# A hybrid attention and Fourier block on one core: the ninth group of the input projection in the order of the others, its chain buffers made earlier, short groups in five accumulators, first-stage raw loads spread

## The chip, the cores and the metric

The kernel runs on one core of a Trainium2 chip. The core has TensorE (PE, matrix products into PSUM banks), VectorE (DVE), ScalarE (ACT), GpSimd (POOL) and SyncE (SP); they run side by side and wait for one another by semaphores. DMA transfers are asked on the queues of SP, ACT and POOL and are carried out by 16 DMA engines that all queues share. The metric is the device time of one execution in microseconds; less is better.

## The reference

One layer of a diffusion block in fp32: 512 latent tokens, 256 context tokens, width 2048.

```python
shift, scale, gate = split(silu(c) @ w_ada + b_ada, 3)          # shift_c, scale_c alike from c_ctx
h  = rmsnorm(x, norm_g) * (1 + scale) + shift                    # 512 x 2048
hc = rmsnorm(ctx, norm_g) * (1 + scale_c) + shift_c              # 256 x 2048
p  = h @ w_in                                                    # 2048 -> 9216: q, k, v, za, ub, zb, ga, gb
kc, vc = (hc @ w_in[:, k and v])                                 # context keys and values
q, k = rope(rmsnorm(q)), rope(rmsnorm(k))
attn = attention(q, [k, kc], [v, vc])                            # 12 query heads, 4 key heads
y_a  = (attn * silu(za)) @ w_proj_a
y_b  = (fft2(ub) * silu(zb)) @ w_proj_b                          # FNet, real part
y    = (sigmoid(ga) * y_a + sigmoid(gb) * y_b) @ w_out
out  = rmsnorm(x + gate * y, final_g)
```

## The kernel before

All products run in three passes: each fp32 weight is split into a high and a low part (`whi` by ACT, line 181, `wlo` by DVE, line 182), and `mm3` (lines 337 to 339) adds hi·hi, hi·lo and lo·hi in PSUM. A raw weight tile (`wr`, 128 x 1024, 0.5 MB) is loaded to one of a few raw slots, split, and used by 12 matmuls; that is a *piece*, and four pieces are a *product*.

The input projection is done in groups of 1024 columns, each as a Winograd form of Strassen's 2x2 scheme with seven products (`PRODUCTS`): P1, Q5, P2, Q6, P7, Q3, Q4. `ORDER` is U (the ninth group, which holds ub and zb), 0 to 2 (queries), 3 and 4 (gates), 5 (keys and values, with the context's), 6 and 7 (gates). The right-hand sides of P1, Q5, Q6 and Q4 are running sums of the four blocks of the weight: w00, then + w01, + w11, + w10. They lie in four *chain* buffers R0 to R3, one for each piece. w00 is loaded plainly, w01 is loaded raw and added by DVE (line 266), w11 and w10 are added by accumulating DMA transfers on POOL's queue (line 287) as soon as the chain's former state has been split. P7's right-hand side is a raw w00 minus the chain (DVE, line 272). P2 and Q3 take raw tiles as they are.

Groups 3, 6 and 7 (`EARLY`) are *short*: what depends on P1 and P2 alone was computed in the first stage, so that they have five products, and their chain's w00 was loaded ahead.

A product's four pieces add up in a pair of PSUM banks. PSUM has room for two pairs under the name `x` and two under `y`. In U the pair `x` takes P1 and then P2 on top of it, and `y` takes Q5 and then Q6, with a copy by ACT between (lines 875 and 880). At the end of a product `early_end` (short groups) or the code above it combines pairs, copies and results.

The first stage computes the modulation vectors from w_ada (`wa` tiles of 1 MB, line 490, on POOL's queue), the norm of x, and h in 16 row blocks kb; x lies in a tile `xt`. Between the blocks TensorE runs the early work for the short groups; its raw tiles are asked on ACT's queue (`load_more`, with `may` as the number that may be asked), and `form_row` (lines 641 to 650) makes the first forms of x for kb from 8 on. `warm` issues matmuls that nobody reads. When the stage is over, `xt`'s pool is closed, the chain buffers are made in its room, and POOL asks their w00 for U (line 738).

The order of TensorE's work is that of the program. On the other engines a scheduler orders the work; `issue_after` pins one instruction behind another. `look` and the raw slots set how far ahead a piece is asked and split; `get` asks for more whenever a piece is used.

In Q4 of the last group TensorE also transposes the keys of the first head (line 1167), into a pair `x`.

## Time and profile before

| what | us |
|---|---|
| median of 3 runs | 1374.88 (1367.93 to 1375.35) |
| the profiled execution | 1372.4 |
| its span | 1370.6 |
| TensorE busy | 1295.0 (94%) |
| DVE busy | 1008.1 (74%) |
| ACT busy | 704.1 (51%) |
| mean granted TensorE clock | 0.983 |

The first stage ends near 152 us, and U near 239; groups 0 to 2 run to about 466, group 3 to about 530, group 4 to 605, group 5 to 740, group 6 to 801, group 7 to 857. The Fourier branch, attention and the output projections follow.

A row of a timeline has the start, the length, the engine, the line, the operation, what it writes and reads, the shapes, and in brackets how long the engine had been idle before it and what ended that. A row of windows has for each engine the busy time and the number of instructions, the granted clock (1.00 is full), the busy share of the DMA engines, and GB/s.

### The profile page before, as it was taken

Reading aid. Unit: us, or ns where it says so; the run is one execution under the profiler, and the core shown is the slowest. Engines: PE = TensorE matmul, PEld = TensorE weight load, DVE = VectorE, ACT = ScalarE, POOL = GpSimd, SP = SyncE. Lnnn points to the kernel's source line nnn. Section 1 sums busy time; section 2 is a strip of 40 time slices with the busy share of each in tenths; the row PEclk is TensorE's granted clock in tenths of the full one; section 3 lists DMA queues with packets and bytes.
Section 4 is the critical chain, followed back from the end, with each engine's and each line's share of the span. In section 5 each row is a group of like instructions: output and inputs, shape, how many; then the busy total and the mean of one; then the engine's idle time right before and its main releaser. Section 6 shows DMA issues by size and latency. Waiting matters only on the chain.

```text
span 1370.6 us, 17532 instructions
## 1 busy us (share of the span) xinstructions
PE 1295.0 (94%) x6444; PEld 1047.1 (76%) x6444; DVE 1008.1 (74%) x1307; ACT 704.1 (51%) x1120; POOL 195.1 (14%) x273
## 2 busy tenths in 40 slices
PE   6889989999999989999999898999999999999997
PEld 4555668888888868878887676788888888888885
DVE  3447688678888778856767578588888867978676
ACT  4343544555555535444333445476766644665544
POOL 0111010101111120100102111001110122121210
PEclk9999999999999999999999999999999999999999
DMA  9999878788988887988788997437873599998985
GB/s 384 416 350 419 291 195 253 191 254 215 255 227 254 304 221 242 291 283 223 194 283 240 264 291 220 179 105 230 261 269 123 156 267 230 241 235 223 215 214 169
DMA packets 109623, 338.46 MB, mean 247 GB/s; under 512 B 10465, under 2 KB 33633, under 8 KB 105441
## 3 DMA queue, kind: packets, MB, share of 16 engines
q0 software_dynamic: 34464, 138.96, 41.9%
q1 hardware_dynamic: 47712, 158.01, 32.4%
q10 hardware_dynamic: 27360, 40.38, 8.1%
q8 instruction: 50, 0.82, 0.2%
q14 instruction: 37, 0.30, 0.1%
HBM read 300.60 MB, written 36.71 MB: 246 GB/s over the span
## 4 chain that ended last, share of the span: by engine, by line
PE 73%; DMA 9%; DVE 8%; issue 5%; ACT 3%; POOL 1%; SPq 0%; ACTq 0%; DVEq 0%; POOLq 0%
PE banks L337 10%; PE banks L338 10%; PE banks L339 10%; PE x L338 6%; PE x L337 6%; PE x L339 6%; PE y L337 5%; PE y L338 5%; PE y L339 5%; DMA R<-in_w_g 3%; DMA wr<-in_w_g 3%; PE banks L1397 2%; PE pd L597 2%; DVE wlo L182 2%; DMA wa<-in_w_ss 1%
## 5 line engine op out<-in xcount | busy, mean ns | idle before, releaser
L182 DVE TENSOR_TENSOR wlo<-wr,whi 128x1024 fp32r<-128x1024 f32 (+1 forms) x130 | 157.5, 1214 | 81.9 <-ACT whi L181 81.6
L181 ACT ACTIVATE whi<-R 128x1024 fp32r<-128x1024 f32 x133 | 140.5, 1059 | 144.4 <-PE banks L339 47.2
L182 DVE TENSOR_TENSOR wlo<-R,whi 128x1024 fp32r<-128x1024 f32 x133 | 162.1, 1223 | 60.3 <-ACT whi L181 59.9
L181 ACT ACTIVATE whi<-wr 128x1024 fp32r<-128x1024 f32 (+1 forms) x130 | 136.4, 1051 | 129.3 <-PE y L339 38.6
L337 PE MATMUL banks<-whi,s 128*128 128x512 f32 x396 | 157.8, 399 | 3.2 <-DVE s L1232 2.2
L338 PE MATMUL banks<-wlo,s 128*128 128x512 f32 x396 | 155.9, 394 | 0.0
L339 PE MATMUL banks<-whi,s 128*128 128x512 f32 x396 | 155.8, 394 | 0.0
L338 PE MATMUL x<-wlo,s 128*128 128x512 f32 x360 | 143.0, 397 | 8.7 <-DVE wlo L182 8.7
L337 PE MATMUL x<-whi,s 128*128 128x512 f32 x360 | 142.3, 395 | 2.6 <-ACT whi L181 2.0
L339 PE MATMUL x<-whi,s 128*128 128x512 f32 x360 | 141.8, 394 | 0.0
L287 POOL DMA_DIRECT2D R<-in_w_g x72 | 61.8, 862 | 465.4 <-DVE wlo L182 266.9
L337 PE MATMUL y<-whi,s 128*128 128x512 f32 x304 | 119.6, 393 | 7.5 <-ACT ev L880 6.8
L339 PE MATMUL y<-whi,s 128*128 128x512 f32 x304 | 119.0, 392 | 0.6 <-DVE s L182 0.6
L338 PE MATMUL y<-wlo,s 128*128 128x512 f32 x304 | 119.1, 392 | 0.4 <-DVE wlo L182 0.4
L181 ACT ACTIVATE s<-wr 128x512 fp32r<-128x512 f32 (+3 forms) x105 | 67.8, 671 | 72.1 <-DMA wr<-cf_d 22.8
L181 ACT ACTIVATE s<-R 128x512 fp32r<-128x512 f32 (+1 forms) x94 | 60.6, 663 | 61.5 <-DMA R<-in_w_g 18.9
L182 DVE TENSOR_TENSOR s<-wr,s 128x512 fp32r<-128x512 f32 (+3 forms) x105 | 75.9, 746 | 22.0 <-ACT s L181 21.4
L337 PEld LDWEIGHTS banks<-whi,s 128*128 128x128 f32 x396 | 75.0, 189 | 18.7 <-issue 2.6
L338 PEld LDWEIGHTS x<-wlo,s 128*128 128x128 f32 x360 | 68.8, 191 | 25.0 <-DVE wlo L182 10.9
L339 PEld LDWEIGHTS banks<-whi,s 128*128 128x128 f32 x396 | 74.9, 189 | 15.8
L338 PEld LDWEIGHTS banks<-wlo,s 128*128 128x128 f32 x396 | 75.1, 190 | 14.1 <-DVE wlo L182 0.2
L182 DVE TENSOR_TENSOR s<-R,s 128x512 fp32r<-128x512 f32 (+1 forms) x94 | 67.1, 734 | 21.4 <-ACT s L181 21.3
(291 smaller groups left out, 2829.3 us busy)
## 6 DMA issues: line engine op xcount, KB each, us to landing
wr<-in_w_g SPq DMA_DIRECT2D x131, 512.0 KB, 5.4
R<-in_w_g POOLq DMA_DIRECT2D x88, 512.0 KB, 7.4
wa<-in_w_ss POOLq DMA_DIRECT2D x26, 1024.0 KB, 11.3
wr<-in_w_gate SPq DMA_DIRECT2D x32, 512.0 KB, 5.5
wr<-in_w_o SPq DMA_DIRECT2D x24, 512.0 KB, 7.9
R<-in_w_o POOLq DMA_DIRECT2D x24, 512.0 KB, 9.1
wr<-in_w_early ACTq DMA_DIRECT2D x21, 512.0 KB, 9.5
R<-in_w_g SPq DMA_DIRECT2D x20, 512.0 KB, 5.2
```

The source lines that it names most:

```text
L181: first = nc.scalar.activation(hi, src, ACT.Copy)
L182: return first, nc.vector.tensor_tensor(lo, src, hi.bitcast(F32), op=ALU.subtract)
L287: nc.gpsimd.dma_start(chain[e.pc], e.nxt, accum_op=ALU.add)
L337: nc.tensor.matmul(o, ah, bh, start=start, stop=False, skip_group_check=cont)
L338: nc.tensor.matmul(o, ah, bl, start=False, stop=False, skip_group_check=cont)
L339: nc.tensor.matmul(o, al, bh, start=False, stop=stop, skip_group_check=cont)
L597: nc.tensor.matmul(acc[32 * j : 32 * j + 32, :256], c2[:, n, :], w[:, k, :], start=h == 0 and k < 4, stop=h == 1 and k > 3)
L1397: nc.tensor.transpose(tp[:, k * P : (k + 1) * P], p[:, k * P : (k + 1) * P], ident)
```

## The change

1. U takes the order of the other groups, with P2 behind Q5. The forms that are split in U (`between`) move with it. Its P1 becomes a piece of stage 0 like the others, whose w00 goes straight to the chain buffer.
2. `xt` becomes two tiles, rows 0 to 3 and 8 to 11 in the pool `xa`, the others in `pa`. At kb 12 `xa` is closed and the chain buffers are made in its room. Their w00 for U is asked on SP's queue behind the last use of `xa`'s rows, in kb 11, and behind two raw tiles for P2 of U, which come first on that queue. POOL's four loads at the end of the stage are gone.
3. Short groups run Q3, Q5, Q6, P7, Q4, each in a pair of its own (Q3, Q6 and Q4 in `x`, Q5 and P7 in `y`). `early_end` takes six DVE operations in place of five and two ACT copies. w10 goes to the chain behind P7's subtraction. The loads for the Fourier branch move along, and the context's tokens in group 3 are worked on in the four pieces of Q6 in place of every other piece of Q3 and Q5.
4. In the first stage the raws that a row block asks are pinned behind that block's ACT operation and are no longer counted one by one. Two raw loads that ACT had asked at 0.7 us, for pieces used at kb 11, go with the others of kb 8. Eight warming matmuls stand at the start and none within the first modulation. `wacc`, where they write, is another bank.

```diff
 OUT_GROUP = ("P1", "P2", "Q5", "Q6", "P7", "Q3", "Q4")
-EARLY_GROUP = ("Q3", "Q5", "P7", "Q6", "Q4")
+EARLY_BANK = {"Q3": "a", "Q5": "b", "Q6": "d", "P7": "c", "Q4": "a"}
+EARLY_GROUP = ("Q3", "Q5", "Q6", "P7", "Q4")
...
-    return EARLY_GROUP if g in EARLY else OUT_GROUP if g == U else ONE_GROUP
+    return EARLY_GROUP if g in EARLY else ONE_GROUP
...
-    if n % 2 == 0 and 0 <= n < 8:
-        return "cn", n // 2
+    if 8 <= n < 12:
+        return "cn", n - 8
...
-                stream(key, [w[a, b, pc] for a, b in what], 1024, 2, pc=r, nxt=part(3) if off and g not in EARLY else None,
-                       off=off)
-            elif (name, g) == ("P1", U):
-                stream(key, [part(0)], 1024, 2, pc=r)
+                stream(key, [w[a, b, pc] for a, b in what], 1024, 2, pc=r, nxt=part(3) if off else None, off=off)
...
-                elif name == "Q6" and g in EARLY:
-                    todo[-1].nxt = part(3)
...
+        if kb == CHAIN_AT:
+            xa.close()
+            rc = ctx.enter_context(tc.tile_pool(name="rc", bufs=1, reuse_waits="tile"))
+            chain.extend(rc.tile([P, 1024], F32, name=f"R{pc}") for pc in range(4))
+        return ins
...
+        warm(8)
         norm_first()
         modulate(0)
-        warm(1)
         columns(0)
...
-                used = sum(r for a in ahead for r in [len(a.raws)])
-                may[0] = sum(p[1] for p in raw_pools) - used
-                load_more()
-                assert not may[0], (kb, may[0])
+                may[0] = 8
+                with tc.issue_after(act):
+                    load_more()
+                may[0] = 0
...
-    for pc in range(4):
-        nc.gpsimd.dma_start(chain[pc], w_g[len(KINDS)][0, 0, pc])
-        left[pc] = 1
...
-            if name == "Q5":
-                self.Y = self.new()
-                nc.scalar.copy(self.Y, a)
+            if name == "Q6":
+                sub(self.X, a, self.X)
+                self.V, self.Y = self.new(), self.new()
+                add(self.V, self.acc["b"], self.X)
+                add(self.Y, self.acc["a"], self.V)
+                self.done(0, 1, self.Y, self.Y)
             elif name == "P7":
-                self.V = self.new()
-                nc.scalar.copy(self.V, a)
-            elif name == "Q6":
+                sub(self.V, self.V, a)
+                self.done(1, 1, self.V, self.V)
                 sub(self.X, a, self.X)
-                sub(self.V, self.X, self.V)
-                self.done(1, 1, self.V, self.V)
-                sub(self.Y, self.X, self.Y)
-                nc.vector.tensor_tensor(self.X, self.acc["a"], self.X, op=ALU.add)
-                self.done(0, 1, self.X, self.X)
             elif name == "Q4":
...
-                    sub(self.Y[:, t, :], a[:, t, :], self.Y[:, t, :])
-                self.done(1, 0, self.Y, self.Y)
+                    add(self.X[:, t, :], a[:, t, :], self.X[:, t, :])
+                self.done(1, 0, self.X, self.X)
```

On TensorE in U, the last matmuls of the product ahead of Q6 and the first of Q6, before (`x` and `y` are pairs of banks, `s_240` and the like are split weights or forms of x; the numbers tell tiles apart, and lines are one or two further in the changed kernel):

```order
L338 MATMUL y_1465<-s_370,s_1372 128x512
L339 MATMUL y_1465<-s_369,s_1373 128x512
L337 MATMUL y_1465<-s_369,s_1372 128x512
L338 MATMUL y_1465<-s_370,s_1372 128x512
L339 MATMUL y_1465<-s_369,s_1373 128x512
L337 MATMUL y_1465<-whi_1490,s_1528 128x512
L338 MATMUL y_1465<-wlo_1491,s_1528 128x512
```

The same place in the changed kernel:

```order
L338 MATMUL x_1300<-s_377,s_1178 128x512
L339 MATMUL x_1300<-s_378,s_1178 128x512
L340 MATMUL x_1300<-s_377,s_1179 128x512
L338 MATMUL x_1300<-s_377,s_1178 128x512
L339 MATMUL x_1300<-s_378,s_1178 128x512
L340 MATMUL x_1300<-s_377,s_1179 128x512
L338 MATMUL y_1387<-whi_1490,s_1528 128x512
L339 MATMUL y_1387<-wlo_1491,s_1528 128x512
```

Before, Q6 follows Q5 in the same pair; now P2 stands ahead of it, in the other pair.

On DVE in group 6, from the last addition to the chain for Q5 on, before (L272 is P7's subtraction, `R_1278` to `R_1281` are the chain buffers):

```order
L266 TENSOR_TENSOR R_1281<-R_1281,wr_5516 128x1024
L272 TENSOR_TENSOR wr_5536<-R_1278,wr_5536 128x1024
L182 TENSOR_TENSOR wlo_5520<-R_1281,whi_5519 128x1024
L272 TENSOR_TENSOR wr_5555<-R_1279,wr_5555 128x1024
L182 TENSOR_TENSOR wlo_5540<-wr_5536,whi_5539 128x1024
L272 TENSOR_TENSOR wr_5574<-R_1280,wr_5574 128x1024
L182 TENSOR_TENSOR wlo_5559<-wr_5555,whi_5558 128x1024
```

The same place now (L273 is the subtraction, `R_1060` to `R_1063` the chain):

```order
L267 TENSOR_TENSOR R_1063<-R_1063,wr_5518 128x1024
L183 TENSOR_TENSOR wlo_5522<-R_1063,whi_5521 128x1024
L183 TENSOR_TENSOR wlo_5541<-R_1060,whi_5540 128x1024
L183 TENSOR_TENSOR wlo_5559<-R_1061,whi_5558 128x1024
L183 TENSOR_TENSOR s_249<-R_1062,s_248 128x2x256
L183 TENSOR_TENSOR s_378<-R_1062,s_377 128x2x256
L273 TENSOR_TENSOR wr_5538<-R_1060,wr_5538 128x1024
L183 TENSOR_TENSOR s_498<-R_1063,s_497 128x2x256
L183 TENSOR_TENSOR s_651<-R_1063,s_650 128x2x256
L183 TENSOR_TENSOR wlo_5613<-wr_5538,whi_5612 128x1024
```

Q6's four splits of the chain come first now, and P7's subtractions behind them.

On TensorE in group 7, around the transposes of the keys (`ident`), before and then now:

```order
L339 MATMUL x_5980<-whi_6175,s_907 128x512
L337 MATMUL x_5980<-whi_6175,s_906 128x512
L1167 MATMUL x_6158<-ident,wr_6052 128x128 x6
L338 MATMUL x_5980<-wlo_6176,s_906 128x512
L339 MATMUL x_5980<-whi_6175,s_907 128x512
```

```order
L339 MATMUL y_6076<-s_378,s_1462 128x512
L340 MATMUL y_6076<-s_377,s_1463 128x512
L1169 MATMUL x_6161<-ident,wr_6051 128x128 x6
L338 MATMUL x_6182<-s_497,s_782 128x512
L339 MATMUL x_6182<-s_498,s_782 128x512
```

They stood within Q4's second piece and stand between P7 and Q4 now.

68 lines of the change are left out of this document (37 added, 31 removed).

## The prediction

> **What bounds the kernel now.** I read the page first (shares, the chain that ended last), then TensorE's timeline for every pause longer than 0.2 us, then for each pause the engine that ended it, then windows and the DMA view.
>
> ```profile
> span 1370.6 us, 17532 instructions
> PE 1295.0 (94%) x6444; PEld 1047.1 (76%) x6444; DVE 1008.1 (74%) x1307; ACT 704.1 (51%) x1120; POOL 195.1 (14%) x273
> PE 73%; DMA 9%; DVE 8%; issue 5%; ACT 3%; POOL 1%; SPq 0%; ACTq 0%; DVEq 0%; POOLq 0%
> ...
> R<-in_w_g POOLq DMA_DIRECT2D x88, 512.0 KB, 7.4
> ```
>
> TensorE is the bound, and time can only come from its pauses. These are the ones that the change touches:
>
> ```profile
> 164.22 0.50 PE L337 MATMUL x<-s,s 128*128 128x512 f32 x1 [1.10 <-ACT ev L875]
> 193.07 0.79 PE L337 MATMUL y<-whi,s 128*128 128x512 f32 x1 [6.80 <-ACT ev L880]
> 499.75 0.79 PE L337 MATMUL x<-s,s 128*128 128x512 f32 x1 [5.79 <-ACT s L181]
> 763.92 0.79 PE L338 MATMUL x<-wlo,s 128*128 128x512 f32 x1 [5.73 <-DVE wlo L182]
> 821.51 0.50 PE L338 MATMUL x<-wlo,s 128*128 128x512 f32 x1 [1.23 <-DVE wlo L182]
> 852.13 1.51 PE L1167 MATMUL x<-ident,wr 128*128 128x128 f32 x6 [6.06 <-issue]
> ```
>
> The first two are in the ninth group U, the next three in the products P7 of the short groups 3, 6 and 7, the last at the key transposes in Q4 of group 7. What stood behind them:
>
> ```profile
> 187.13 1.15 ACT L181 ACTIVATE s<-R 128x512 fp32r<-128x512 f32 x2 [4.00 <-DMA R<-in_w_g]
> 192.02 0.99 ACT L880 COPY ev<-y 128x1024 f32<-128x1024 f32 x1
> 497.81 1.23 DVE L272 TENSOR_TENSOR wr<-R,wr 128x1024 f32<-128x1024 f32 x1 [4.24 <-DMA wr<-in_w_g]
> 752.75 1.23 DVE L272 TENSOR_TENSOR wr<-R,wr 128x1024 f32<-128x1024 f32 x1 [0.81 <-DMA R<-in_w_g]
> 761.50 1.23 DVE L272 TENSOR_TENSOR wr<-R,wr 128x1024 f32<-128x1024 f32 x1 [6.39 <-DMA wr<-in_w_g]
> 819.10 1.22 DVE L272 TENSOR_TENSOR wr<-R,wr 128x1024 f32<-128x1024 f32 x1 [2.62 <-DMA R<-in_w_g]
> 850.81 1.22 DVE L930 TENSOR_TENSOR ev<-x,ev 128x1024 f32<-128x1024 f32 x1
> ```
>
> In U, Q6 writes the bank that Q5 filled; ACT is to copy it (192.02) but sat at 187.13 on a split of Q6's weights whose chain DMA was late. In groups 3 and 6 a raw tile for P7's subtraction came late. The "issue" of 852.13 names nobody; the transposes write a bank that Q3 held until DVE's last use of it, at 850.81 plus 1.22 us.
>
> A pause costs more than its length, as the granted clock drops behind it. An undisturbed window has 46 matmuls in 10 us, so I count what is missing (windows of TensorE alone: length, busy and number, granted clock, DMA share, GB/s):
>
> ```profile
> 170.00:180.00 10.00, 10.00 (x46) 1.00 1.05 298
> 180.00:190.00 10.00, 6.27 (x28) 1.00 0.87 238
> 190.00:200.00 10.00, 6.93 (x21) 0.66 0.26 40
> ...
> 490.00:500.00 10.00, 4.21 (x18) 0.89 0.85 264
> 500.00:510.00 10.00, 10.00 (x35) 0.77 0.79 198
> ...
> 750.00:760.00 10.00, 7.16 (x28) 1.00 1.04 267
> 760.00:770.00 10.00, 6.08 (x19) 0.66 0.71 246
> ...
> 840.00:850.00 10.00, 6.07 (x29) 0.97 1.01 339
> 850.00:860.00 10.00, 7.87 (x30) 0.69 0.76 259
> ```
>
> At 4.6 matmuls a us: U (92-49)/4.6 = 9.3 us, group 3 (92-53)/4.6 = 8.5, group 6 (92-47)/4.6 = 9.8, the keys (92-59)/4.6 = 7.2. A product of 48 matmuls is 48/4.6 = 10.4 us.
>
> **U in the common order.** These windows name all engines (PE, weight loads, DVE, ACT, POOL). P2 now stands between Q5 and Q6, and Q5 between P1 and P2. Each copy gets 10.4 us before its bank is written again, and each chain DMA (7.4) a product in which to land. I take off all of 9.3 and the 1.1 of 164.22: -10.4 (bounds -10.4 and 0). Against it: the work of U closes up, and DVE's stays.
>
> ```profile
> 170.00:240.00 70.00, 62.57 (x266) 50.92 (x265) 60.99 (x70) 33.28 (x42) 6.83 (x8) 0.95 0.80 227
> ```
>
> DVE is busy 61.0 of these 70 us; its operations of 1.22 us start 1.14 apart when nothing waits, so that is some 57 us net, beside 266/4.6 = 57.8 us of TensorE's. DVE has next to no room, but it runs pieces ahead and some of it is for group 0. I add 1.5 (bounds 0 and 6). U: -8.9.
>
> **Short groups, Q6 ahead of P7.** P7's raw tile is asked where it was, and is used a product later: the 4.24 and 6.39 us of DVE's wait lie inside 10.4. Group 3 gives 8.5, group 6 9.8, group 7 its 1.2. What is late next: Q6 needs the chain with w11 added, by the accumulating DMA that starts when Q5's piece has been split, and Q6 now follows Q5 directly. Before, P7's subtraction stood there and waited for the same DMA: 0.81 in group 6 and up to 2.62 in group 7. Q6 needs one DVE operation less than P7 behind that DMA. I put 0.5, 1.5 and 2.0 us on groups 3, 6 and 7 (bounds 0 and U's 9.3 each). The same holds for P7 and Q4, where the DMA now starts behind the subtraction, which DVE does during Q6; before it was Q6 and Q4, without a pause, so nothing. Five banks instead of four cost one DVE operation of 1.2 us more and two ACT copies less a group; DVE is the busier engine but at two thirds to three quarters in groups 6 and 7 (the windows below), so nothing.
>
> **The key transposes** stand behind P7 now, and Q3's bank is free when Q6's three operations are done, during P7: -7.2 (bounds -7.2 and 0; the keys' load is asked some 10 us earlier relative to its use than the transposes need, and could become the wait).
>
> **DMA room in groups 6 and 7.** Three of these gains lie in one stretch:
>
> ```profile
> 741.00:801.00 60.00, 52.69 (x216) 41.45 (x217) 39.79 (x43) 26.83 (x33) 9.55 (x13) 0.94 0.93 267
> 801.00:857.00 56.00, 48.71 (x211) 39.83 (x210) 42.34 (x44) 27.35 (x34) 9.50 (x13) 0.94 0.86 246
> ```
>
> The DMA engines are busy 0.93*60 + 0.86*56 = 104 of 116 us. The TensorE gains are 9.8 + 1.2 + 7.2 - 3.5 = 14.7; what is left would be 101 us, for 104 us of transfers at a share of 1.00 (105 at the 1.05 seen above would fit). I take 12.5 of the 14.7 (bounds 5 and 18). Group 3 (-8.5 + 0.5 = -8.0) has 0.85 and 0.79 in its windows and room.
>
> **Stage 1.** Two early raw loads (1 MB) no longer start at 0.7 us, warming matmuls leave the chain, and the raws of a row are asked only behind that row's ACT work.
>
> ```profile
> 17.56 1.13 PE L591 MATMUL pb<-pick,ones 128*128 128x256 f32 x4
> 19.37 0.65 PE L591 MATMUL pb<-pick,ones 128*128 128x256 f32 x2
> 20.95 0.70 PE L591 MATMUL pb<-pick,ones 128*128 128x256 f32 x2
> ...
> 0.00:72.00 72.00, 52.73 (x376) 33.31 (x376) 31.63 (x68) 30.18 (x61) 10.64 (x27) 0.98 0.99 400
> 95.00:140.00 45.00, 42.52 (x314) 25.82 (x314) 30.88 (x67) 16.61 (x27) 5.38 (x10) 1.00 1.00 403
> ```
>
> The three rows are 2.5 us, and 1 MB at 400 GB/s is 2.6 us of a stretch in which the DMA engines are full; both shorten the same stretch: -2.5 (bounds -5 and 0). Against it, the raw split at kb 9 is asked about 99.9 (behind ACT's copy at 99.52) in place of a row earlier. ACT's timeline, and the DMA view of 95 to 140 (packets, MB, share; and the median us to landing):
>
> ```profile
> 99.52 0.37 ACT L613 COPY ado<-pd 128x256 f32<-128x256 f32 x1 [3.02 <-PE pd L597]
> 103.79 1.05 ACT L181 ACTIVATE whi<-wr 128x1024 fp32r<-128x1024 f32 x1
> 106.81 0.37 ACT L613 COPY ado<-pd 128x256 f32<-128x256 f32 x1 [1.97 <-PE pd L597]
> ...
> q0 software_dynamic: 1643, 11.89, 65.0%
> q10 hardware_dynamic: 1707, 6.21, 34.6%
> ...
> wr<-in_w_early ACTq DMA_DIRECT2D x4, 512.0 KB, 11.8
> ```
>
> At 11.8 us it lands at 111.7 where ACT wants it at 103.8; one load fewer ahead of it on ACT's queue (0.5 MB at 6.21 MB/45 us = 3.8 us) makes that 107.9, ACT is held 4.1 us, has 1.97 idle, and TensorE gets its copy 2 us late: +2 (bounds 0 and 6). Then six raws of 0.5 MB for U (chain buffers and P2) come on SP's queue between about 117 and 140, into full DMA engines (1.00); before only five stood on ACT's. Two MB more are 5 us at 403 GB/s, of which most falls into the idle DMA time behind 140; I add 1.5 (bounds 0 and 7.4, below). Stage 1: +1.0. The loads that POOL issued at the start of U fall away; their cover is counted in U.
>
> The last fence's two queue rows show one packet of each in turn (1643 and 1707, of 7.2 and 3.6 KB). The Trainium skill, "DMA: Bandwidth & Descriptors", section "Queues, rings and completion order", says that each engine goes round the queues that have work, a packet at a time; the trace agrees. By it a third queue would take a turn too, and the sum's 1.5 would be 7.4.
>
> **Sum.** -8.9 - 8.0 - 12.5 + 1.0 = -28.4. The profiled execution took 1372.4 us, 2.5 under the median of the runs (1374.88): 1344.0 against its own time, 1346.5 against the median; I take 1345.
>
> **Rivals.**
> 1. Stage 1 pays. If SP's queue takes turns with the other two, `wa` has 7.2 of 14.4 KB, 201 GB/s in place of 264; while 3.1 MB go through at 101 GB/s (31 us), 1.95 MB are missing, 7.4 us at 264 GB/s. With kb 9 at its bound of 6, stage 1 is -2.5 + 13.4 = +10.9 and the time 1355. For it: the share of 1.00. Against: ACT's queue empties near 130, and a held TensorE lets `wa` catch up. Chance 0.11.
> 2. The change doesn't do what it says: P7's raws are late again, since the slots come free with Q5's adds as before and full DMA engines (1.04 at 750) push them back by a product. Groups 3 and 6 keep their pauses: 8.0 and about 7, time 1360. Against: the same half MB on POOL's queue lands in 7.4, within the 10.4 that it now has. Chance 0.09.
> 3. Slower: the chain DMA between neighbours. Q5-Q6 and P7-Q4 in three groups are six places like the one in U that cost 9.3. Six such are 56 us: 1345 + 56 - 4 (counted) = 1397. It decides against the change from (1374.9 + 6.9 - 1341)/6 = 6.8 us a place, that is where the DMA takes about 17 us. For it: it is U's own mechanism, in fuller stretches. Against: 0.81 to 2.62 us of wait in the same place before. Chance 0.10.
>
> **How the numbers follow.** The forecast (1337 to 1352) has 0.64, the rivals 0.11, 0.09 and 0.10; 0.06 is left for mixtures that end within 0.5%, 6.9 us, about what a measurement of this kernel can tell from no change. Faster: 0.64 + 0.11 + 0.09 = 0.84. 1335 to 1362 holds the forecast and the first two rivals with their bounds, a little over 8 in 10.
>
> **What would show it.** Right: no pause over 1 us between 155 and 240; none at P7 in groups 3 and 6; the transposes without a wait; first matmul of U within 2 us of before. Wrong: a wait of Q6's first pieces for R (rival 3), DVE at 95% in U with TensorE waiting for `wlo`, ACT at the split of kb 9 or TensorE for `wa` behind 117 (rival 1), L272 waiting for `wr` (rival 2).

## The result and the profile after

The changed kernel takes 1350.84 us (median of 3 runs, 1349.89 to 1357.18) where the kernel before took 1374.88: a ratio of 0.9858 with a 95% interval of 0.9811 to 0.9905. The forecast was 1345, its range 1335 to 1362, and "faster" had 0.84. The sign is right, and the time lies 6 us above the forecast. A repeat gave 1349.5 us (6 runs, 1347.95 to 1359.55) beside 1372.27, again 0.9858 (0.9828 to 0.9887).

The page of the changed kernel, its span, shares and chain that ended last:

```profile
span 1349.1 us, 17543 instructions
PE 1295.0 (96%) x6452; PEld 1046.1 (78%) x6452; DVE 1011.0 (75%) x1310; ACT 697.0 (52%) x1114; POOL 193.7 (14%) x269
PE 67%; DMA 14%; DVE 7%; issue 6%; ACT 4%; POOL 1%; SPq 0%; ACTq 0%; POOLq 0%; DVEq 0%
```

TensorE is as busy as before to the tenth of a microsecond (1295.0), so the 21.5 us of the span are idle time that TensorE no longer has. A matmul that runs slowly behind a pause counts as busy, so the equal sum does not say that no slow time went or came: U's granted clock rose (0.95 to 1.00 in 170 to 240), and that of the first stage fell. Where the time came out is read from the starts of the same instruction in both traces:

| instruction | before | after | shift | of this stage |
|---|---|---|---|---|
| first gate store (line 676), end of the first stage | 151.0 | 156.3 | +5.3 | +5.3 |
| a uz store behind U (line 957, 959 after) | 241.6 | 235.5 | -6.2 | -11.5 |
| first key store in group 5 (line 1024, 1026 after) | 674.1 | 661.8 | -12.3 | -6.1 |
| last such store | 742.6 | 730.1 | -12.5 | -0.2 |
| first sigmoid of the Fourier part (line 1229, 1231 after) | 869.6 | 848.7 | -20.9 | -8.4 |
| end | 1370.6 | 1349.1 | -21.5 | -0.6 |

The parts in between are read from the matmuls. The changed kernel has eight more, all ahead of U, so from U on each matmul of the kernel before is paired with the one that stands eight places further. Of the -6.1, group 3 has -4.6 and groups 4 and 5 have -1.5. Of the -8.4, group 6 has -7.5, and group 7 with the keys has -6.2 up to its last matmul (861.8 before, 835.6 after); at the entry to the Fourier part, between that matmul and the first sigmoid, 5.3 us are lost again. The forecast had put +1.0 (first stage), -8.9 (U), -8.0 (group 3) and -12.5 (groups 6 and 7) for these places, and nothing for the entry.

TensorE's timeline after: its longer pauses, without those that the kernel before had too (for `wa` near 60 and 70, and one at 862).

```profile
18.84 0.66 PE L599 MATMUL pd<-wa,c 128*32 128x256 f32 x4 [4.95 <-ACT root L529]
...
110.63 0.48 PE L621 MATMUL pd<-ident,ado 128*128 128x128 f32 x1 [3.76 <-ACT ado L613]
...
483.83 0.49 PE L338 MATMUL y<-s,s 128*128 128x512 f32 x1 [2.58 <-ACT s L182]
...
814.35 0.50 PE L339 MATMUL y<-wlo,s 128*128 128x512 f32 x1 [1.73 <-DVE wlo L183]
...
839.83 0.47 PE L338 MATMUL x<-s,s 128*128 128x512 f32 x1 [3.62 <-DVE ev L923]
```

The pauses that the change aimed at are gone: none of over 1 us between 155 and 480, where U had 6.80 and 1.10; none at P7 of groups 3 and 6, which had 5.79 and 5.73; none at the key transposes, which had 6.06. Five others are new or longer. The first two lie in the first stage (the place of the first had 1.35 us of wait before), the third at Q6 of group 3 (in the place of its P7), the fourth at P7 of group 7, the fifth at the Fourier part's first product, which had not waited before.

What stood behind them, ACT's timeline first:

```profile
17.00 0.63 ACT L182 ACTIVATE whi<-wr 128x512 fp32r<-128x512 f32 x1 [4.33 <-DMA wr<-in_w_early]
17.54 0.29 ACT L529 ACTIVATE root<-pd,eps_t 32x64 f32<-32x64 f32 x1
...
109.26 1.06 ACT L182 ACTIVATE whi<-wr 128x1024 fp32r<-128x1024 f32 x1 [6.14 <-DMA wr<-in_w_early]
...
481.59 0.63 ACT L182 ACTIVATE s<-R 128x512 fp32r<-128x512 f32 x1 [3.82 <-DMA R<-in_w_g]
...
482.13 1.04 ACT L1092 ACTIVATE wr<-wr 128x1024 f32<-128x1024 f32 x1
```

and the same place at the start in the kernel before:

```profile
15.25 1.26 ACT L527 ACTIVATE root<-pd,eps_t 32x64 f32<-32x64 f32 x4 [2.70 <-PE pd L547]
16.87 0.63 ACT L181 ACTIVATE whi<-wr 128x512 fp32r<-128x512 f32 x1 [0.36 <-DMA wr<-in_w_early]
```

The first weight lands at the same time in both, near 16.9. But the split that needs it now stands ahead of the norm's root on ACT, and the root, whose sums TensorE had finished at 13.9, waits behind it until 17.5. The fifth pause is DVE's:

```profile
834.23 1.23 DVE L183 TENSOR_TENSOR wlo<-wr,whi 128x1024 fp32r<-128x1024 f32 x1 [2.39 <-ACT whi L182]
837.26 1.22 DVE L183 TENSOR_TENSOR wlo<-wr,whi 128x1024 fp32r<-128x1024 f32 x1 [1.80 <-ACT whi L182]
838.40 0.68 DVE L923 TENSOR_TENSOR ev<-x,ev 128x512 f32<-128x512 f32 x1
```

Q4 of the short groups now has a pair of banks `x` of its own. DVE frees it with the addition of line 923, and that addition stands behind two splits of the gate branch's weights, which ACT hands over late. The 3.62 us of pause and the half speed behind it (a matmul every 0.43 us in place of 0.23 from 840.6 to 843.6) make the 5.3 us that the entry loses.

U and group 6, windows (length; PE, weight loads, DVE, ACT, POOL busy with their numbers; granted clock; DMA share; GB/s):

```profile
170.00:240.00 70.00, 70.00 (x311) 57.95 (x310) 64.36 (x74) 38.56 (x47) 5.92 (x7) 1.00 0.81 241
...
720.00:780.00 60.00, 58.39 (x248) 45.76 (x248) 47.93 (x54) 27.73 (x45) 13.86 (x17) 1.00 0.94 276
```

In U TensorE has 311 matmuls in 70 us against 266 before, at a full clock, and DVE is busy 64.4 of the 70 us without TensorE ever waiting for it.

### The profile page after: what moved, and what is told of

It is laid out like the page before. It is cut to its first block, busy times and chain, and to the rows that moved or that the text cites. A ratio compares the mean times of both kernels' runs of the same rounds, so it can differ in the third digit from the quotient of the medians.

```text
span 1349.1 us, 17543 instructions
## 1 busy us (share of the span) xinstructions
PE 1295.0 (96%) x6452; PEld 1046.1 (78%) x6452; DVE 1011.0 (75%) x1310; ACT 697.0 (52%) x1114; POOL 193.7 (14%) x269
## 4 chain that ended last, share of the span: by engine, by line
PE 67%; DMA 14%; DVE 7%; issue 6%; ACT 4%; POOL 1%; SPq 0%; ACTq 0%; POOLq 0%; DVEq 0%
PE banks L338 10%; PE banks L339 9%; PE banks L340 9%; PE x L338 5%; PE x L340 5%; PE x L339 5%; DMA R<-in_w_g 5%; PE y L339 5%; PE y L338 5%; PE y L340 5%; DMA wa<-in_w_ss 2%; PE banks L1399 2%; DVE wlo L183 2%; DMA wr<-in_w_g 2%; DMA wr<-in_w_pab 2%
## 5 line engine op out<-in xcount | busy, mean ns | idle before, releaser
L183 DVE TENSOR_TENSOR wlo<-wr,whi 128x1024 fp32r<-128x1024 f32 (+1 forms) x128 | 154.7, 1214 | 87.1 <-ACT whi L182 86.9
L338 PE MATMUL x<-whi,s 128*128 128x512 f32 x360 | 140.9, 391 | 1.6 <-ACT whi L182 0.9
L340 PE MATMUL x<-whi,s 128*128 128x512 f32 x360 | 140.1, 389 | 0.0
L183 DVE TENSOR_TENSOR s<-wr,s 128x512 fp32r<-128x512 f32 (+3 forms) x101 | 73.2, 747 | 19.4 <-ACT s L182 18.7
L338 PEld LDWEIGHTS x<-whi,s 128*128 128x128 f32 x360 | 67.7, 188 | 17.0 <-ACT whi L182 2.2
## 6 DMA issues: line engine op xcount, KB each, us to landing
wa<-in_w_ss POOLq DMA_DIRECT2D x26, 1024.0 KB, 10.6
```

Of the source, the lines that this page charges most:

```text
L183: return first, nc.vector.tensor_tensor(lo, src, hi.bitcast(F32), op=ALU.subtract)
L338: nc.tensor.matmul(o, ah, bh, start=start, stop=False, skip_group_check=cont)
L340: nc.tensor.matmul(o, al, bh, start=False, stop=stop, skip_group_check=cont)
```

## The experiments

Every kernel here is the changed one with the edit shown. The first stage and the last 500 us scatter by a few microseconds from one execution to the next in code that no edit touches: among seven profiles with the same first stage (the first, its repeat, and those of e4, e5, e6, e7 and e10) the end of that stage lies between -1.7 and +5.1 us of the first profile. So each verdict rests on the edited stretch: TensorE's matmuls are the same 6452 in all these kernels, and the shift of the matmul of the same number against the changed kernel's profile is read at both ends of the stretch. The total stands beside it. e7 and e10 have a single execution each.

**e4: U in its old order.**

```diff
-    return EARLY_GROUP if g in EARLY else ONE_GROUP
+    return EARLY_GROUP if g in EARLY else OUT_GROUP if g == U else ONE_GROUP
```

(with the map of `between` put back to suit)

> The changed kernel with the ninth group's products in the order of before (P1, P2, Q5, Q6), all else of the change kept. Theory A (the gain in the ninth group comes from the order: a product between Q5 and Q6 covers the copy of the bank and the chain transfer): a pause of 4 us or more comes back at Q6 between 180 and 210 with the granted clock dropping behind it, and the time rises by 9 to 12, to 1360 to 1363. Rival B (the gain comes from where the chain buffers lie and from loads no longer issued on POOL at the group's start): the pause stays under 1.5 us and the time rises by less than 3, to 1351 to 1354.

Measured: 1356.4 us (1351.76 to 1360.91). U takes 5.5 us longer (the shift goes from +5.1 at 155 to +10.6 at 200). TensorE:

```profile
174.64 0.50 PE L338 MATMUL x<-s,s 128*128 128x512 f32 x1 [1.10 <-ACT ev L879]
...
198.88 0.50 PE L338 MATMUL y<-whi,s 128*128 128x512 f32 x1 [2.18 <-ACT ev L884]
```

Both pauses of before are back in their places, but the second has 2.18 us where it had 6.80. The size lies between the two theories: the order accounts for 5.5 of U's 11.5 us when the rest of the change is kept.

**e8: the chain's first block asked by POOL.** The chain buffers stay where the change put them.

```diff
+            elif (name, g) == ("P1", U):
+                stream(key, [part(0)], 1024, 2, pc=r)
...
     pa.close()
+    for pc in range(4):
+        nc.gpsimd.dma_start(chain[pc], w_g[len(KINDS)][0, 0, pc])
+        left[pc] = 1
```

> The changed kernel, the ninth group in its new order, but with the group's chain filled as before: POOL asks the four chain loads when the first stage has ended, and P1's pieces come as four raw loads. Run beside the one with the old order: that one lost 5.5 us in the ninth group, and 6.0 us of the 11.5 are left to explain. Theory A (the other half is these loads: asked at the start of the group they stand in full DMA engines and every later chain transfer comes late behind them): a pause of 1 us or more comes back in the ninth group and the group is 4 to 7 us longer, time 1354 to 1358. Rival B (with a product between Q5 and Q6 the late chain is covered, and the two causes don't add): under 1.5 us in the ninth group; the first stage is shorter by up to 1.5 us, since no chain load goes beside wa; time 1349 to 1351.

Measured: 1351.91 us (1347.99 to 1358.15); U takes as long as in the changed kernel (the shift is +1.6 at 158 and at 235), with no pause. That is B's result, but the experiment was weaker than meant: though the loads stand behind the first stage in the program, POOL asked them 20 to 28 us before its end, since the room was free.

```profile
129.34 0.55 POOL L743 DMA_DIRECT2D R<-in_w_g  x1 [0.69 <-DVE adr L625]
...
135.93 1.60 POOL L743 DMA_DIRECT2D R<-in_w_g  x3
```

Which queue asks is of no account for U, then, when it asks that early. When it asks was left to the next kernel.

**e9: the chain's room free only at the end of the first stage.** As e8, and:

```diff
-    xts = [p.tile([P, 2, 8, 256], F32, name=uid("xt")) for p in (xap, pap)]
+    xts = [p.tile([P, 2, 8, 256], F32, name=uid("xt")) for p in (pap, xap)]
...
-        if kb == CHAIN_AT:
-            xa.close()
-            rc = ...
...
+    xa.close()
     pa.close()
+    rc = ...
```

> The changed kernel, the ninth group in its new order, with the chain buffers back in the room of the latent rows that are read last, so that POOL can ask the four chain loads only when the first stage ends, as before the change; P1's pieces come as raw loads. The kernel with the chain asked by POOL, but already 20 us earlier in the free room, showed no pause in the ninth group, and the one with the old order and the early chain lost 5.5 us. Theory A (order and early chain each cover the other: with a product between Q5 and Q6 even the late chain is in time): the ninth group is within 1.5 us of the changed kernel. Theory B (each carries its own half): a pause of 1 us or more comes back and the group is 4 to 7 us longer. On the first stage: if its end is set by the sum of the loads (1.6 MB more went through it after the change, 4.3 us at its 371 GB/s), the first gate store comes 3 to 6 us earlier than in the changed kernel's profile, since 2 MB are asked later; if the copies' own chain sets it, by less than 1.5 us. Time 1345 to 1350 by A with the first of these, 1350 to 1353 by A with the second, 1353 to 1358 by B.

Measured: 1364.54 us (10 runs, 1359.03 to 1371.45). U takes 11.6 us longer (-0.3 at 158, +11.3 at 170), all of it at one place, the second product. TensorE, DVE and POOL there:

```profile
174.51 0.79 PE L339 MATMUL x<-wlo,s 128*128 128x512 f32 x1 [8.87 <-DVE wlo L183]
```

```profile
164.16 1.22 DVE L267 TENSOR_TENSOR R<-R,wr 128x1024 f32<-128x1024 f32 x1 [8.17 <-issue]
166.88 1.23 DVE L267 TENSOR_TENSOR R<-R,wr 128x1024 f32<-128x1024 f32 x1 [1.50 <-DMA R<-in_w_g]
169.36 1.22 DVE L267 TENSOR_TENSOR R<-R,wr 128x1024 f32<-128x1024 f32 x1 [1.25 <-DMA R<-in_w_g]
172.10 1.23 DVE L267 TENSOR_TENSOR R<-R,wr 128x1024 f32<-128x1024 f32 x1 [1.52 <-DMA R<-in_w_g]
```

```profile
156.53 2.13 POOL L742 DMA_DIRECT2D R<-in_w_g  x4 [21.70 <-ACT ev L677]
```

Neither theory had this. Q5 needs w00 + w01 in all four buffers. In the old order it is the third product and the buffers have two products' time; in the new order it is the second. The loads asked at 156.5 arrive one by one into DMA engines that are full (0.98 from 160 to 174.5), and each addition waits for its own. With the three other corners U's table is complete: old order and late chain is the kernel before (11.5 us longer than the changed one; its first stage differs too), old order and early chain 5.5, new order and late chain 11.6, new order and early chain 0. The order alone would have gained nothing; the room for the chain is its condition.

On the first stage, 2 MB less went through it, and its end lies 0.3 us earlier than in the changed kernel's first profile. That comparison hides what the loads for U cost, since the pause at kb 9 scatters and was 6.17 us here against 3.76. Read from ACT's copy of kb 14 to the end of the stage, against the kernel before, the changed kernel loses 1.0 us, and the seven profiles named above lose 0.7 to 2.0; each has a wait for the last `wa`, of 0.5 to 1.8 us, such as this one of the changed kernel:

```profile
147.49 1.07 PE L599 MATMUL pd<-wa,c 128*32 128x256 f32 x16 [0.79 <-DMA wa<-in_w_ss]
```

In e9 that wait is gone and the stretch loses nothing (0.0); in e8, where POOL asks the chain loads on the queue of `wa`, it is gone too, and 0.3 us are lost. The last `wa` landed 13.8 us after it was asked in the changed kernel, 11.4 in e8 and 10.1 in e9. So the loads for U appear to cost the first stage about 1 us, at its very end, though e8 and e9 have one profile each.

**e5: the short groups in their old order,** with their old banks, last steps and Fourier places.

```diff
-EARLY_GROUP = ("Q3", "Q5", "Q6", "P7", "Q4")
+EARLY_GROUP = ("Q3", "Q5", "P7", "Q6", "Q4")
```

(and all that hangs on it put back as before)

> The changed kernel with the four groups that have five products in the order and banks of before (P7 ahead of Q6, four banks, ACT's two copies at the end, forms of the Fourier part where they were), the ninth group and the first stage as changed. Theory A (the parts of the change add up): the pauses at P7 of groups 3 and 6 come back with 5 us or more each, and those at the key transposes too, and the time rises by 12 to 15, to 1363 to 1366. Rival B (the pauses of before at these places were set by a late stage in front of them, which the ninth group's change moves): under 5 us in all, 1351 to 1356. Rival C (DMA room bounds this stretch, so that what the ninth group gains is lost here again): more than 18, above 1369.

Measured: 1363.11 us (1359.73 to 1367.39). The pauses return at once:

```profile
493.88 0.80 PE L338 MATMUL x<-s,s 128*128 128x512 f32 x1 [5.62 <-ACT s L182]
...
754.31 0.79 PE L339 MATMUL x<-wlo,s 128*128 128x512 f32 x1 [5.93 <-DVE wlo L183]
...
843.45 0.37 PE L1170 MATMUL x<-ident,wr 128*128 128x128 f32 x1 [4.64 <-issue]
```

The shift goes from +1.6 at 470 to +3.1 at 740, +12.5 at 800 and +12.7 at the end: 11.1 us for the short groups, a little under theory A's 12 to 15. Of the 11.1, groups 3 to 5 have 1.5, group 6 has 9.4, and all behind it 0.2. The losses are this part's own, not a late stage's in front of them.

**e7: the context tokens' pieces back where they were.** It asks whether ACT's square (482.13 above), which the change moved into Q6, makes the pause of group 3.

```diff
-    if 8 <= n < 12:
-        return "cn", n - 8
+    if n % 2 == 0 and 0 <= n < 8:
+        return "cn", n // 2
```

> The changed kernel with the context tokens' norm pieces of the first short group back under Q3 and Q5, where they stood before, in place of Q6. Theory A (the pause of 2.58 us at Q6 of that group is mostly the chain transfer, asked 1.7 us late behind a root of POOL's, and only 1.0 us of it is ACT's square between two halves of one split): the pause becomes 1.2 to 1.9. Rival B (the pieces themselves make it): it goes under 0.6. Rival C (the same work, earlier, delays the chain as much or more): 2.5 or more.

Measured: 1354.45 us, one execution. The pause is 3.16 us, though no square stands between the halves of the split. The outcome is rival C's, but it does not clear the square wholly. In the changed kernel 2.32 us lie between the landing of the transfer (481.51) and TensorE's first matmul of Q6 (483.83): two splits with the square between them. In e7 it is 1.80 us, as TensorE's operand comes out of the third split; but the transfer took 8.20 us in place of 7.47 and landed 1.1 us later in the stage. The square's place is worth 0.5 us here, and the landing more. POOL's root still stands ahead of the chain transfer:

```profile
472.12 1.69 POOL L983 TENSOR_TENSOR small<-small,mhalf 128x8 f32<-128x8 f32 x1
473.77 0.91 POOL L288 DMA_DIRECT2D R<-in_w_g  x1
```

**e10: without that root.** One query norm's reciprocal root is left out of the computation.

```diff
-        root_of(ss)
+        turned.append(half)
+        if len(turned) != 6:
+            root_of(ss)
```

> The changed kernel without POOL's two operations of one query norm, those that stand ahead of the chain transfer for Q6 of the first short group (the reciprocal root of that norm is left out of the computation); the order on ACT, DVE and TensorE is the changed kernel's. Theory A (the transfer is asked 1.6 us late because of these operations, and that is what is left of the pause once ACT's square is out of the way): POOL issues it at 472.3 to 472.6 on the changed kernel's scale, the split's 3.82 us of wait becomes 2.0 to 2.4 and TensorE's pause of 2.58 us becomes 0.7 to 1.3. Rival B (the transfer lands by what the DMA engines have to do, not by when it is asked): it takes longer by what it is asked earlier, and the pause stays above 2.0.

Measured: 1353.78 us, one execution, the stretch 1.8 us later on the clock of the trace. POOL, ACT and TensorE:

```profile
474.58 0.86 POOL L288 DMA_DIRECT2D R<-in_w_g  x1 [4.32 <-DVE wlo L183]
```

```profile
483.16 0.63 ACT L182 ACTIVATE s<-R 128x512 fp32r<-128x512 f32 x1 [3.44 <-DMA R<-in_w_g]
```

```profile
485.40 0.49 PE L338 MATMUL y<-s,s 128*128 128x512 f32 x1 [2.36 <-ACT s L182]
```

POOL now issues as soon as DVE has split the piece, at 474.58 - 1.8 = 472.8 against 474.04, and the data is there 483.16 - 474.58 = 8.6 us later, where the changed kernel had 481.59 - 474.04 = 7.6. Of 1.3 us, 0.2 arrive; the pause stays at 2.36. Rival B holds, as far as one execution shows it: the DMA engines are at 0.96 to 0.99 in these 8 us. The other profiles agree. On the changed kernel's scale the ten that have the square in its place and this order of the short groups asked the transfer at 473.7 to 474.6, and it landed at 480.5 to 481.7; e10 asked at 472.8, and it landed at 481.3, among them. In all eleven TensorE's first matmul came 2.32 or 2.33 us behind the landing, so the pause (1.55 to 2.76 us) follows the landing. That what the DMA engines have to do sets it is the reading that fits; no run took load from them there.

**e6: the gate branch's weights held behind Q4's last addition.**

```diff
+                if e.key[0] == "pab" and q4_end:
+                    line.enter_context(tc.issue_after(q4_end[0].ins))
...
-            if e is turn[0] or e.key[0] != "V":
+            if e is turn[0] or e.key[0] != "V" and not (held and e.key[0] == "pab"):
```

> The changed kernel with the two early splits of the gate branch's weights in the last group held until DVE has done Q4's last addition, which then comes ahead of them; this also moves the first Fourier forms by a few places on DVE and ACT. Theory A (the Fourier part's first product waits for Q4's bank, because Q4's addition stands behind those splits on DVE): TensorE's wait of 3.62 us there goes under 1.5, and the half speed behind it goes too: 3 to 5 us, time 1346 to 1348. Rival B (behind the addition the next thing is late, the first forms or the held weights): the wait moves to another line within 30 us and the time is 1349.5 to 1352.

Measured: 1351.2 us (1350.47 to 1352.49). DVE adds at once, and TensorE no longer waits at the Fourier part's first product:

```profile
835.65 1.29 DVE L925 TENSOR_TENSOR ev<-x,ev 128x512 f32<-128x512 f32 x2 [4.40 <-PE x L342]
836.85 2.35 DVE L183 TENSOR_TENSOR wlo<-wr,whi 128x1024 fp32r<-128x1024 f32 x2
```

The shift goes from +1.0 at 835.6, the last matmul of Q4, to -4.2 at 848: the mechanism is the one named, and it is worth 5.2 us there, as much as the entry lost. (The +1.0 arose at 814 to 818, where the same pause of 1.73 us at P7 is followed by a granted clock of 0.60 in e6 and of 1.00 in the changed kernel's profile.) But at 960 the shift is -1.5 and at 1060 +0.6; the waits at 858 and 866 are 0.5 and 0.3 us longer, the matmuls behind the first run at a clock of 0.61 to 863, and a few other waits are new. The total shows no gain: rival B's outcome, by several small waits and a slower clock behind one rather than by one wait.

**e1: the root ahead of the first split.**

```diff
-            nc.scalar.activation(r[k], acc[k, t * 64 : t * 64 + 64], ACT.Sqrt, ...)
+            root_last[0] = nc.scalar.activation(r[k], acc[k, t * 64 : t * 64 + 64], ACT.Sqrt, ...)
...
-            split_piece(ahead[0])
+            with tc.issue_after(root_last[0].ins):
+                split_piece(ahead[0])
```

> The changed kernel with one dependency of order more: ACT's first weight split waits for the norm's first square root, so that the root stands ahead of the split as it did before the change. Theory A (the start is lost to this order, because the split waits 4.33 us for its load and the root waits behind it): TensorE's first product with wa waits under 1.5 us for the root in place of 4.95, its 16 matmuls take 1.1 us each and not 1.94, and ACT's copy of kb 0 comes 3.5 us earlier. Theory A1: the loads bound the rest of the first stage, the copies meet the changed kernel's again by kb 5 and the time is 1350 to 1351. Theory A2: ACT and TensorE bound the first stage, the 3.5 us stay and the time is 1347 to 1348. Rival B (the start is late because the load itself is late): kb 0 moves by less than 1 us.

Measured: 1350.33 us (1345.52 to 1351.69).

```profile
14.73 0.42 PE L602 MATMUL pd<-wa,c 128*32 128x256 f32 x4 [1.35 <-ACT root L531]
...
37.51 0.65 PE L602 MATMUL pd<-wa,c 128*32 128x256 f32 x4 [4.49 <-DMA wa<-in_w_ss]
```

The start is mended: 1.35 us of wait in place of 4.95, and full speed behind it (granted clock 1.00 from 14 to 25, where the changed kernel had 0.50 from 18.8 to 25). ACT's copy of kb 0 comes 6.7 us earlier, more than the 3.5 expected. Then TensorE waits for `wa` at 37.5, and the first stage ends 0.3 us earlier than the changed kernel's. A1 and not A2: the loads take the gain back.

**e2: the two postponed raws a row earlier.**

```diff
-RAW_LATER, HL_LATER = 8, {3: 0, 7: 1}
+RAW_LATER, HL_LATER = 7, {3: 0, 7: 1}
```

> The changed kernel with the two postponed raw loads of the first stage asked a row of kb earlier, so that the raw that ACT splits at kb 9 is asked some 7 us before it is now. Theory A (the stall at kb 9 is the time that this load takes after it is asked, and the 5 us lost there stay lost): ACT's wait of 6.14 us at the split and TensorE's 3.76 us at the copy of kb 9 go under 1.5, the first gate store comes 4 to 5 us earlier, time 1346 to 1347. Rival B (the load takes the DMA share that wa would have, so that the wait goes to wa): the waits of 6.14 and 3.76 go, but TensorE waits for wa by 3 us or more longer between kb 8 and 15, and the gate store moves by less than 1.5 us; time 1349.5 to 1351.

Measured: 1353.48 us (1352.17 to 1354.83). The waits of 6.14 and 3.76 us at kb 9 are gone; one row of blocks earlier a smaller one stands,

```profile
95.07 0.50 PE L338 MATMUL pb<-whi,s 128*128 128x512 f32 x1 [2.89 <-ACT s L637]
```

and the first gate store comes at 153.70 in place of 156.34: -2.6 us, between the two theories. Against the kernel before, the copies stand at +1.0 from kb 9 to kb 14; the other 1.7 us come at the end, where TensorE waits 1.51 us for `wa`. The time doesn't show it. In this execution the shift goes from -3.0 at 812 to +3.9 at the end, in code that is the same; the section on the hardware shows the largest piece of it.

**e3: the raw loads of the first stage not pinned.**

```diff
-                with tc.issue_after(act):
-                    load_more()
+                load_more()
```

> The changed kernel with the raw loads of the first stage free to be asked as early as the buffers allow, as before the change, in place of behind the row's ACT work. Theory A (pinning the loads is what made the first stage 5 us longer): the first split no longer waits 4.3 us at the start, the split at kb 9 waits under 2 us, and the first gate store comes 4 to 8 us earlier than in the changed kernel; time 1345 to 1347. Rival B (the early loads take the room of wa, as they did before the change, and wa waits again): the start is 3 us earlier or more but the gain is lost by kb 15, and the gate store moves by less than 2 us; time 1349 to 1352.

Measured: 1355.57 us (1349.33 to 1356.47). Theory A fell at the start: TensorE still waits 4.51 us for the root, since the order of split and root is the same and the first weight again lands at 16.9. The stall at kb 9 is gone, `wa` is late instead (2.33 at 59.4 and 2.68 at 63.2), and the gate store comes 2.1 us later. To ask the raws early costs at least what it saves. That is nearest to rival B, though its early start did not come and the median lies above its range.

**e11 and e12: three edits together, and the changed kernel once more.** e11 has the edits of e1, e2 and e6.

```diff
-RAW_LATER, HL_LATER = 8, {3: 0, 7: 1}
+RAW_LATER, HL_LATER = 7, {3: 0, 7: 1}
...
+            with tc.issue_after(root_last[0].ins):
+                split_piece(ahead[0])
...
+                if e.key[0] == "pab" and q4_end:
+                    line.enter_context(tc.issue_after(q4_end[0].ins))
```

> The changed kernel with three of the edits that each took a new pause away: the norm's root ahead of the first split, the two postponed raws of the first stage asked a row of kb earlier, and the gate branch's weights held behind Q4's last addition. Alone they moved the first gate store by -0.3, -2.6 and nothing, and the Fourier part's start by 0, 0 and -3.0, against the changed kernel's profile. Theory A (each pause is on the path for itself): the first gate store comes 4 to 8 us earlier than in the repeat of the changed kernel, the Fourier part's first product waits under 1 us, and the time is 5 us or more below the repeat. Theory B (behind each pause the next thing is late by as much: wa after the start, the forms after Q4): the gate store moves by less than 3 us, and the time is within 3 us of the repeat.

> The changed kernel once more, beside the one with three edits and the kernel before on the same chip. It should be at 0.982 to 0.988 of the kernel before; its first stage shows how far the wait at kb 9 varies from one execution to another (3.76 us in the first profile, 4.4 to 6.8 in four profiles of kernels with the same first stage).

Measured: e11 takes 1345.86 us (1342.19 to 1348.27), 0.9807 of the kernel before (0.9784 to 0.983); e12 1349.5 us (1347.95 to 1359.55), 0.9858 (0.9828 to 0.9887). e11's first gate store comes 3.1 us earlier than in the first profile and 1.4 earlier than in e12; the Fourier part's first product starts without a wait,

```profile
834.53 0.47 PE L340 MATMUL x<-s,s 128*128 128x512 f32 x1
```

against

```profile
838.28 0.47 PE L338 MATMUL x<-s,s 128*128 128x512 f32 x1 [1.83 <-DVE ev L923]
```

in e12. Of theory A the Fourier part's wait went as said, but not the gate store's 4 us nor the time's 5; of theory B the gate store holds, and its bound of 3 us on the time is passed by a little, with 3.6 us between the medians. The two intervals just touch, so that e11 is the fastest kernel of this study, by some 0.3%, which these runs make likely but not certain. The wait at kb 9 was 4.44 us in e12; over the seven profiles it ran from 3.76 to 6.81.

## Why the prediction was right, and where it was not

The sign and the range came from the mechanism that the prediction named: a pause is a bank or a buffer that is needed one product too early, and a product in between covers it. e5 shows it for the short groups (11.1 us), e4 and e9 for U. That the total came within 6 us of the forecast is in part luck. The first stage, group 3 and the entry to the Fourier part came out 13.0 us worse than forecast (4.3, 3.4 and 5.3), while U, groups 6 and 7, and groups 4 and 5 came out 5.5 us better; the gain in groups 4 and 5, 1.7 us, had no term in the sum. Term by term:

- **U, -8.9 forecast, -11.5 measured.** The 10.4 us of pauses went, and 1.1 us more that no term counted. The step that failed is the 1.5 us against it, DVE's want of room: DVE was busy 64.4 of 70 us and TensorE never waited. And the prediction credited the order alone ("P2 now stands between Q5 and Q6"). e9 shows that this order with the chain asked when it was asked before is 11.6 us slower, because Q5 moves from third to second place. The prediction followed what the move does for Q6 and not what it asks of Q5; the chain's new room, of which it said only that "the loads that POOL issued at the start of U fall away", was half of the gain with the old order and the condition of all of it with the new.
- **Group 3, -8.0 forecast, -4.6 measured.** P7's pause went as said (-7.6). The failed step is "what is late next", put at 0.5 us and measured at 3.0: Q6's chain transfer, asked when Q5's piece has been split, took 7.5 us to land, and TensorE waited 2.58 us for it and the splits behind it. It is the third rival's mechanism at one of six places and in a third of its size. Asking sooner does not bring the landing forward (e10), and ACT's square holds some 0.5 us of the pause (e7); that the full DMA engines hold the rest fits all profiles and was not tested.
- **Group 6, -8.3 before the cap, -7.5 measured.** Right as worked out, within 1 us.
- **Group 7 and keys, -6.4 before the cap, -6.2 measured; the entry to the Fourier part, nothing forecast, +5.3 measured.** The transposes' pause went as said, with 1.73 us of wait left at P7. The failed step is "Five banks instead of four ... so nothing": with banks of its own, Q4 gives up `x` to the Fourier part only after DVE's addition, which now stands behind two weight splits. The step counted DVE's time and not DVE's order. e6 shows that this alone holds it: with the addition first, 5.2 us come back there. The wait was 1.2 to 5.6 us in other profiles without that edit.
- **DMA room, a cap of 14.7 to 12.5; measured 13.7 for groups 6 and 7, and 8.4 with the entry.** The cap brought the number nearer to 8.4, but not for its reason: up to group 7's last matmul 13.7 of the 14.7 us came, with a DMA share of 0.94 in group 6 (the window above), and e6 won the loss behind it back by order alone.
- **First stage, +1.0 forecast, +5.3 measured in the first profile, +3.6 in the repeat.** Three steps. The start was put at -2.5 by the matmuls taken out; in place of that the root and the first split had changed places on ACT, which the prediction didn't take up: +3.5 us at kb 0. e1 mends that order and has -3.2 there, so what was taken out of the start does give about what was put; but by kb 5 the copies of both are level with those of the kernel before (+0.1), since TensorE waits for `wa`. The stall at kb 9 was named in place and cause, and mis-sized: 2 us were put, where the copies' shift goes from -0.8 to +4.3. The sum had the raw land 8.0 us after it was asked (11.8, less 3.8 for one load fewer ahead of it); asked at 98.75 with three others, it took 10.4 us, and ACT was held 6.14 us in place of 4.1. The late loads of U, put at 1.5 us with a bound of 7.4, cost 1.0 (0.7 to 2.0 over the seven profiles, and nothing in e9, where 2 MB of them come later), about the size that was put. What ended the first stage later is thus mostly kb 9: e2, which mends it, ends 2.6 us earlier than the first profile and 2.7 later than the kernel before. Of that remainder 1.7 us come behind kb 14, with the wait for `wa`, and the 1.0 from kb 9 on stays open.

Of the rivals, the first (the first stage pays) came half true, by the stall that it named; the third queue cost some 1 us and not 7.4. The second fell: no P7 waits for its raw. The third happened at one place. Of the signs that the prediction named for being right, three came, and one did not: U's first matmul is 5.3 us later than before and not within 2.

## What to carry to other kernels

When a product is moved away from the one that it waits for, write down for each product that moves what it needs and how much earlier it now needs it; here the order gained nothing until its second product's operands were asked 20 us sooner (e8 against e9). Read the order of every engine at the place where loads are moved, since a scheduler may put a split that waits for a load ahead of a small operation on which TensorE hangs. When a product gets a bank of its own, look at who frees that bank, and at what stands ahead of the freeing operation on its engine. A pause that was taken away in front of full DMA engines came back here as a wait for the next load (e1, e3), so judge an edit by the shift over the whole stage, and by a repeat, before counting the pause.

## What the runs showed of the hardware

**The same pause costs the clock in one execution and not in another.** At the second step of the Fourier part each of these kernels waits 2.2 to 2.7 us for the same operation. In the changed kernel the matmuls behind it run at full speed, in e2 at half. The windows (columns as above) of the changed kernel and of e2:

```profile
860.00:870.00 10.00, 6.96 (x35) 5.39 (x33) 5.62 (x7) 4.46 (x6) 1.06 (x2) 1.00 0.88 328
```

```profile
860.00:870.00 10.00, 8.95 (x32) 7.40 (x33) 5.30 (x7) 3.73 (x4) 0.53 (x1) 0.66 0.76 285
```

and TensorE's timeline of each:

```profile
862.49 0.47 PE L338 MATMUL banks<-whi,s 128*128 128x512 f32 x1 [2.22 <-DVE s L1234]
```

```profile
861.05 0.77 PE L338 MATMUL banks<-whi,s 128*128 128x512 f32 x1 [2.23 <-DVE s L1234]
861.62 0.63 PE L339 MATMUL banks<-wlo,s 128*128 128x512 f32 x1
862.04 0.63 PE L340 MATMUL banks<-whi,s 128*128 128x512 f32 x1
```

Between 860 and 866 e2 loses 2.8 us on it. The Trainium skill, "TensorE: Matmul & The Clock Gate", in its section on the clock gate, says that activity is watched in windows of about 3.4 us that run free of the program; that the same pause should fall differently in different executions agrees with it, though no run here shows the window. The same section of the Trainium skill has the clock fall after at least one idle window; here 2.2 us of pause were enough in e2, where the granted clock from 861 to 867 is 0.50. At P7 of group 7 it was 1.73 us: behind that pause the clock is 1.00 in the changed kernel's profile and in e1's, and 0.60 to 0.62 in those of e6, e11 and e12. This is one reason why the total hides an edit of 3 us in this kernel. The changed kernel's first profile had full speed at both places, so an edit that is compared with it can look worse than it is, in e6 by 1.6 and 1.5 us.

**Asking earlier did not bring the data earlier.** With the DMA engines at 0.96 to 0.99, an accumulating transfer of half a megabyte that was asked 1.3 us sooner landed 0.2 us sooner (e10), within the 1.2 us over which the landing scatters in ten profiles that asked it later.
